# Second layer of a hybrid attention/RWKV-7 kernel: norm behind centring, Gram products earlier, T's blocks turned directly behind them

## The chip, the cores and the metric

The kernel runs on one core of one Trainium2 chip. The metric is the device time of one execution in microseconds (us); the time before is the median of three runs, 2163.39 us (2161.89 to 2163.66). The engines are called PE (matrix multiplications), DVE (VectorE), ACT (ScalarE), POOL (GpSimd) and SP (which issues most loads). Each takes its instructions strictly in the order of the program, and waits at an instruction until what it reads, and the place that it writes, are ready.

## The reference

The reference is a trunk of two residual layers over 512 positions of 2048 channels. Layer 0 is gated differential attention; the change does not touch it. Layer 1 is RWKV-7 time mixing with 32 heads of 64 channels:

```
h = rms_norm(x);  p = h @ w_in;  p = p + (token_shift(p) - p) * mu
r, k, v, g, dw, da = split(p)             # receptance, key, value, gate, decay, rate
for t in range(T):                        # for each head, S is 64 x 64
    sa = S @ a_t
    S  = S * w_t + outer(sa, b_t) + outer(v_t, k_t)
    y_t = S @ r_t
y = (y - mean) * rsqrt(var + eps) * gn_w + gn_b     # over the 64 channels of a head
y = y + sum(r * k * r_k) * v
out = x + (y * silu(g)) @ w_out
```

## The kernel before, in words

Layer 1 goes over 16 pairs of heads, j = 0 to 15; a pair's 128 channels fill the partitions. Each pair needs four projections (keys, receptances, values, gate) of 2048 input channels onto 128 outputs. `proj` makes one out of 48 matmuls of 128x512 into a tile `pp` (16 blocks of input channels, three products each, since both sides are split into a high and a low half; `wh` and `wl` on ACT and DVE make the halves of the weights). These projections are most of PE's work, and all else is hung between their matmuls.

**The recurrence** is done in 8 chunks of 64 positions. For a pair, `gram` makes the products of keys and queries (tile `gp`, 32 matmuls, L1136) from the tiles `BK` and `AR`; ACT copies the 32x32 blocks that the inverse needs to `LP` (L1144) and the rest to `G` (L1150). `t_solve` inverts 64x64 triangular blocks of all chunks at once, which gives T: it turns the blocks on DVE (`LT`, L1214), does 31 steps of elimination on DVE (two instructions each, L1227 and L1230, with tiles `tmpl` and `Tm`), and turns the result twice (`T1`, L1235; `W`, L1240), which POOL copies into `TT` (L1246). `t_first` and `t_second` (PE products into `px`, L1261 and L1276) complete the inverse's lower blocks. POOL's two `affine_select` of each head (`mask_gram`, L1180 and L1182) zero the part of `G` above the diagonal.

**The scan**, `scan_pair`, then goes through the chunks c = 0 to 7. For each: a product of PE into `sm` (L1353), a copy on ACT (`rhs`, L1356), a product (L1366), a copy on ACT (`VS`, L1368), a product (L1373), and on DVE the new state (L1377, for c = 0 L1380), on which the next chunk's L1353 waits. Between them lie fixed counts of `pp` matmuls, the `gaps`: (7, 8) for the full iterations. POOL copies the state into `SA` (L1361) and scales it (L1364). Behind the last chunk come the outputs Y on PE, `centre` (L1410 to L1412 on DVE, result `yc`) and, called from a later place in the loop, `group_norm` (L1420 on ACT, L1422 to L1426 with the helper's lines 63 to 70 on DVE).

**What sets the order.** Iteration j makes the values' projection of pair j (with the Gram products of j behind its 18th matmul, a hook), the keys' projection of j+1, the gate's of j-3 (from j = 3, the constant LAG), and the receptances' projection of j+1 (with masks, `t_first`, `t_second` and the key norms `norms` of a pair as hooks). At the same time the scan of pair j-1 and the elimination of pair j are stepped by a count of PE's matmuls: each `yield n` in `t_solve` or `scan_pair` means that the next piece is bound to the place n matmuls on. That holds for the program's order. The engines wait for data alone, so DVE works the steps off as early as its own queue lets it. Between these bonds the scheduler picks the order on each engine by priority (`AHEAD`, `SCAN`, `SOLVE` raise it).

`soon(g)` runs pieces that were put off until the first `rhs` copy of a chunk; before, it holds the four `G` copies.

Of the kernel before, what the change touches and what calls it, by code (L numbers as in the profile page):

```python
# [1043 lines left out]
    g.nc.tensor.matmul(out, ones, l[:], start=False, stop=True)  # L1044


def soon(g):
    while g.soon:
        g.soon.pop(0)()


def stage1(g, j, k, up):
# [73 lines left out]
def gram(g, j, p):  # L1126

    nc, w, BK = g.nc, g.work, p.BK
    p.G = w.tile([P, NC_, 2, 2, C], F32, name="G1", tag="G1", bufs=2)
    halves = []  # L1130
    for c0, tag in ((0, "pb"), (4, "pc")):
        gp = [g.ps.tile([P, 512], F32, name="gp", tag=tag, bufs=2) for _ in range(2)]
        halves.append((c0, gp))
        for i in range(4):
            for h, r_ in ((0, slice(0, C)), (1, slice(C, P))):
                m = nc.tensor.matmul(gp[h][:, i * P : (i + 1) * P], BK[r_, c0 + i, :, :], p.AR[r_, c0 + i, :, :],  # L1136
                                     start=True, stop=True)
# [9 lines left out]
    def grams():  # L1147
        for c0, gp in halves:
            for h in range(2):
                nc.scalar.copy(p.G[:, c0 : c0 + 4, :, h, :], gp[h][:].rearrange("p (u x t) -> p u x t", u=4, x=2))  # L1150

    g.soon.append(grams)
    if not j:
        soon(g)


def norms(g, j, p, m):
# [49 lines left out]
def t_solve(g, j, p):  # L1207


    nc, w = g.nc, g.work  # L1210
    NQ = HALF // NG
    yield 9
    LT = w.tile([P, HALF, HALF], F32, name="LT", tag="LT", bufs=1)
    lt = nc.vector.transpose(LT[:].rearrange("p (r c) t -> p t r c", r=NG),  # L1214
                        p.LP[:].rearrange("p c t -> p t c")[:, :, None, :].to_broadcast([P, HALF, NG, NC_]))
    Tm = w.tile([P, NQ, HALF], F32, name="Tm", tag="Tm", bufs=1)
    tmp = w.tile([P, NQ * HALF], F32, name="tmpl", tag="tmpl", bufs=1)
    nc.gpsimd.tensor_copy(Tm[:], g.unit[:])
    n2 = p.n2
    behind(g, lt)  # L1220
    with g.tc.issue_after(lt.ins):
        nc.vector.tensor_scalar(n2[:], n2[:], 1e-24, None, ALU.max)
        nc.vector.reciprocal(n2[:], n2[:])
    for i in range(HALF - 1):
        n, s = HALF - 1 - i, i // NG + 1
        tt = tmp[:, : n * s].rearrange("p (a b) -> p a b", a=s)
        st = nc.vector.scalar_tensor_tensor(tt, LT[:, i : i + 1, i + 1 :].to_broadcast([P, s, n]), n2[:, i : i + 1],  # L1227
                                       Tm[:, 0:s, i : i + 1].to_broadcast([P, s, n]), ALU.mult, ALU.mult)
        behind(g, st)
        nc.vector.tensor_add(Tm[:, 0:s, i + 1 :], Tm[:, 0:s, i + 1 :], tt)  # L1230
# [4 lines left out]
    tt = nc.vector.transpose(p.T1[:].rearrange("p c (q r) -> p q r c", r=NG),  # L1235
                        Tm[:].rearrange("p q (r c) -> p q r c", r=NG))
    p.W = w.tile([P, NC_, HALF], F32, name="W", tag="Tm", bufs=1)
    behind(g, tt)
    yield 4
    tt = nc.vector.transpose(p.W[:], p.T1[:])  # L1240
# [101 lines left out]
def scan_pair(g, j, p, gap, gap_s, others):  # L1342
# [8 lines left out]
    for c in range(NC_):  # L1351
        sm = g.ps.tile([P, 512], F32, name="sm", tag="pa", bufs=1)
        nc.tensor.matmul(sm[:, 0:P], both(p.G[:, c, 0]), both(VS[:, c]), start=True, stop=True)  # L1353
# [12 lines left out]
        nc.tensor.matmul(sm[:, P : P + C], both(g.TT[j % 2][:, c]), rhs[:], start=True, stop=True)  # L1366
        for h, r_ in HEADS:
            nc.scalar.copy(VS[r_, c, h, :], sm[r_, P : P + C])  # L1368
        yield gap
        if c == NC_ - 1:  # L1370
            break
        o = P + C
        nc.tensor.matmul(sm[:, o : o + P], p.BKT[:, c, :], both(VS[:, c]), start=True, stop=True)  # L1373
        for h, r_ in HEADS:
            s_ = sm[r_, o + h * C : o + h * C + C]
            if c:
                g.state = nc.vector.scalar_tensor_tensor(VS[r_, c + 1, h, :], s_, p.gam[r_, c : c + 1], Sg[r_, :],  # L1377
                                                         ALU.mult, ALU.add)
            else:
                nc.vector.tensor_scalar(VS[r_, c + 1, h, :], s_, p.gam[r_, c : c + 1], None, ALU.mult)  # L1380
        if c in others:
            others[c]()
        yield gap_s
    outputs(g, j, p)
    centre(g, p)


def outputs(g, j, p):
# [23 lines left out]
        nc.vector.tensor_sub(p.yc[:, h::2, :], yg, s1[:, :, h : h + 1].to_broadcast([P, NT, C]))  # L1412


def group_norm(g, j, p):
    p.chain.finish(g)
    nc, w, yc = g.nc, g.work, p.yc
    NG = 2 * NT
    sq = w.tile([P, NG, C], F32, name="ysq", tag="thg", bufs=1)
    nc.scalar.activation(sq[:], yc[:], AF.Square)  # L1420
    var = g.small.tile([P, NG], F32, name="var", tag="var")
    nc.vector.reduce_sum(var[:], sq[:], AX.X)  # L1422
# [15 lines left out]
def layer1(g, aps):  # L1438
    nc, tc = g.nc, g.tc
    with ExitStack() as cx:  # L1440
# [7 lines left out]
        def proj(i, j, **k):  # L1448
            return unit_chan(g, [(win, i * D + j * P, P)], P, **k)[0]

        def begin(j):
# [5 lines left out]
            pairs.append(stage1(g, j, shift_mix(g, proj(1, j), P, *mus(g, 1, j), "k", 1), up))  # L1457

        def receptances(j):
            def piece(f, i, p):  # L1460
# [2 lines left out]
                        f(g, i, p)  # L1463
                return follow

            behind = [(39, lambda m: norms(g, j, pairs[j], m))]
            if j:
                behind += [(6, lambda m: [mask_gram(g, pairs[j - 1], h, m) for h in range(2)]),
                           (12, piece(t_first, j - 1, pairs[j - 1])), (33, piece(t_second, j - 1, pairs[j - 1]))]
            return shift_mix(g, proj(0, j, behind=behind), P, *mus(g, 0, j), "r", 1)  # L1470

        begin(0)
# [1 line left out]
        for j in range(D // P):  # L1474
            p = pairs[j]
            if j:
# [18 lines left out]
            stage_v(g, j, p, proj(2, j, behind=hooks))  # L1495
            if j == 0:
                turn_keys(g, p, 0)
                turn_keys(g, p, 4)
                turn_values(g, p)
            if j + 1 < D // P:  # L1500
                begin(j + 1)
            if j >= LAG:
                gated(g, j - LAG, pairs[j - LAG], gate(g, j - LAG, proj(3, j - LAG)))
            if j + 1 < D // P:
                r = receptances(j + 1)
                if j:
                    with tc.high_priority(offset=AHEAD):
                        group_norm(g, j - 1, pairs[j - 1])
# [3 lines left out]
        group_norm(g, j - 1, pairs[j - 1])  # L1512
        gts = [gate(g, j - 1, gps)]

        def last_but_one(m):
# [7 lines left out]
        def all_rows(n, _):  # L1523
            if n >= 4 and len(rows) == KT - 2:
                rows.append(split_row(g, gts[0][:]))
            if n >= KT and len(rows) < KT:
                group_norm(g, j, p)
# [59 lines left out]
def body(ctx, tc, nc, aps):  # L1587
    g = Ctx()
    g.nc, g.tc = nc, tc
    g.last, g.first = None, []  # L1590
    g.chains, g.later, g.soon, g.state, g.solve = [], [], [], None, None
# [38 lines left out]
```

## Time and profile before

| what | before |
|---|---|
| median of three runs | 2163.39 us |
| time of the profiled execution | 2163.93 us |
| its span, first to last instruction | 2162.2 us |
| granted PE clock | 0.998 |
| DVE, slices 20 to 35 of the page's 40 (about 1080 to 1945 us) | 80% busy or more |
| first and last Gram products (L1136) start | 1042.3 and 1914.0 us |

The times in the prediction are microseconds from the start of the span of the profiled execution. A row of the timeline reads: start, duration, engine, line, operation, tile written and tiles read with their shapes, how often in a row, and in brackets the time that the engine sat idle before it and what released it. A `pp` matmul shows with 0.39 us, but they overlap: one starts about 0.23 us after the other.

### The profile page before, as it was taken

The page shows a single profiled execution, that of the slowest core. Times are in us where ns is not written, and L with a number is a line of the kernel's source. Part 1 is how long each engine was busy: PE and PEld are TensorE (multiplying, and loading weights), DVE is VectorE, ACT ScalarE, POOL GpSimd, SP SyncE. Part 2 cuts the span into 40 slices and gives each one's busy share as a digit, 9 for nine tenths or more (in the row PEclk, how much of TensorE's full clock was granted, in tenths as well). Part 3 has the DMA queues.
Part 4 walks back from the last instruction along what each step waited for, and adds up shares of the span by engine and source line. Part 5 has one row for each costly group of instructions (what it writes and reads, how often), then busy time and mean ns, then how long its engine had stood idle before and what let it go on. Part 6 is the DMA issues. An engine that isn't in the chain of part 4 may idle for free.

```text
span 2162.2 us, 34954 instructions
## 1 busy us (share of the span) xinstructions
PE 2130.9 (99%) x12260; PEld 1752.8 (81%) x12260; DVE 1547.3 (72%) x4137; ACT 1125.5 (52%) x2587; POOL 335.2 (16%) x614
## 2 busy tenths in 40 slices
PE   9999999999999999999999999999999999999999
PEld 8888888888888878887777888888888888877887
DVE  5665647465656667457888988888888898887645
ACT  6443434343444455345666666666666666655333
POOL 0000000000000000011133322223333322232001
PEclk9999999999999999999999999999999999999999
DMA  6223232322223365663222233222232222345565
GB/s 196 90 86 100 79 99 87 98 89 88 97 88 97 99 198 182 185 139 87 73 69 65 67 81 85 76 77 76 78 85 77 77 68 79 89 118 186 179 169 120
DMA packets 258624, 225.77 MB, mean 104 GB/s; under 512 B 12336, under 2 KB 220480, under 8 KB 258448
## 3 DMA queue, kind: packets, MB, share of 16 engines
q1 hardware_dynamic: 239504, 188.03, 29.2%
q0 software_dynamic: 10080, 19.50, 4.5%
q10 hardware_dynamic: 8864, 16.01, 2.0%
q8 instruction: 96, 1.57, 0.3%
q14 instruction: 80, 0.66, 0.1%
HBM read 207.50 MB, written 15.99 MB: 103 GB/s over the span
## 4 chain that ended last, share of the span: by engine, by line
PE 85%; DVE 11%; issue 2%; ACT 1%; DMA 1%; POOL 0%; DVEq 0%; ACTq 0%; POOLq 0%
PE pp L129 66%; PE pt L129 5%; DVE wl L116 2%; DVE LT L1214 1%; PE sm L1353 1%; PE o L129 1%; PE sc L129 1%; PE lora L129 1%; PE sm L1373 1%; PE sm L1366 1%; DMA yr<-yd 1%; DVE tmpl L1227 1%; PE Y L1395 1%; DVE Tm L1230 1%; PE pt L346 1%
## 5 line engine op out<-in xcount | busy, mean ns | idle before, releaser
L116 DVE TENSOR_TENSOR wl<-wraw,wh 128x512 fp32r<-128x512 f32 (+1 forms) x636 | 446.9, 705 | 383.7 <-ACT wh L115 374.5
L115 ACT CAST wh<-wraw 128x512 fp32r<-128x512 f32 (+1 forms) x636 | 392.9, 619 | 516.9 <-PE pp L129 407.8
L129 PE MATMUL pp<-wh,hH 128*128 128x512 f32 x1268 | 500.3, 395 | 1.2 <-DVE prmin_rw_mu_dram L234 0.6
L129 PE MATMUL pp<-wh,hL 128*128 128x512 f32 x1268 | 497.6, 393 | 0.0
L129 PE MATMUL pp<-wl,hH 128*128 128x512 f32 x1268 | 497.1, 392 | 0.0
L129 PE MATMUL pp<-hH,wh 128*128 128x512 f32 x1024 | 417.7, 408 | 0.0
L129 PE MATMUL pp<-hH,wl 128*128 128x512 f32 x1024 | 413.3, 404 | 0.0
L129 PE MATMUL pp<-hL,wh 128*128 128x512 f32 x1024 | 413.3, 404 | 0.0
L129 PEld LDWEIGHTS pp<-wh,hH 128*128 128x128 f32 x1268 | 238.3, 188 | 50.0 <-issue 1.6
L129 PEld LDWEIGHTS pp<-wh,hL 128*128 128x128 f32 x1268 | 238.2, 188 | 48.6
L129 PEld LDWEIGHTS pp<-wl,hH 128*128 128x128 f32 x1268 | 238.4, 188 | 46.8
L129 PEld LDWEIGHTS pp<-hH,wh 128*128 128x128 f32 x1024 | 193.2, 189 | 37.8 <-issue 2.0
L129 PEld LDWEIGHTS pp<-hH,wl 128*128 128x128 f32 x1024 | 193.6, 189 | 33.4
L129 PEld LDWEIGHTS pp<-hL,wh 128*128 128x128 f32 x1024 | 193.5, 189 | 32.2
L1361 POOL COPY SA<-VS 64x64 f32<-64x64 f32 x224 | 78.0, 348 | 472.6 <-DVE VS L1377 406.9
L1227 DVE SCALAR_TENSOR_TENSOR tmpl<-LT,n,Tm 128x60 f32<-128x60 f32 (+24 forms) x496 | 136.2, 275 | 13.8
L500 POOL DMA_DIRECT2D frow<-yd x12 | 8.9, 743 | 807.6 <-DVE rs_t L67 675.8
L1230 DVE TENSOR_TENSOR Tm<-Tm,tmpl 128x60 f32<-128x60 f32 (+24 forms) x496 | 114.1, 230 | 13.2
L1356 ACT COPY rhs<-sm 64x64 f32<-64x64 f32 x256 | 52.7, 206 | 61.8 <-PE sm L1353 58.9
L1368 ACT COPY VS<-sm 64x64 f32<-64x64 f32 x256 | 53.0, 207 | 59.1 <-PE sm L1366 48.0
L1353 PEld LDWEIGHTS sm<-VS,G 128*128 128x128 f32 x256 | 45.0, 189 | 29.8 <-PE pp L129 12.9
L1377 DVE SCALAR_TENSOR_TENSOR VS<-sm,gam,Sg 64x64 f32<-64x64 f32 x192 | 54.1, 282 | 18.7 <-PE sm L1373 14.2
(339 smaller groups left out, 3261.9 us busy)
## 6 DMA issues: line engine op xcount, KB each, us to landing
wraw<-in_rw_w_in_dram SPq DMA_DIRECT2D x128, 512.0 KB, 4.0
wraw<-in_da_w_in_dram SPq DMA_DIRECT2D x254, 256.0 KB, 3.0
wraw<-in_da_w_out_dram SPq DMA_DIRECT2D x26, 512.0 KB, 4.4
wraw<-in_rw_w_out_dram SPq DMA_DIRECT2D x26, 512.0 KB, 4.1
yr<-yd SPq DMA_DIRECT2D x28, 256.0 KB, 3.4
frow<-yd POOLq DMA_DIRECT2D x12, 512.0 KB, 6.2
xq<-in_x_dram SPq DMA_DIRECT2D x16, 256.0 KB, 5.0
xd<-xq ACTq DMA_DIRECT2D x16, 256.0 KB, 3.9
```

Source lines behind the costliest of these rows:

```text
L115: nc.scalar.copy(hi[:], raw[:, k : k + n])
L116: nc.vector.tensor_sub(lo[:], raw[:, k : k + n], hi[:].bitcast(F32))
L129: m = nc.tensor.matmul(out, a, b, start=s, stop=e, skip_group_check=skip)
L346: nc.tensor.transpose(pt[:, c * P : (c + 1) * P], t1s[t][:, c * P : (c + 1) * P], g.ident[:])
L1214: lt = nc.vector.transpose(LT[:].rearrange("p (r c) t -> p t r c", r=NG), p.LP[:].rearrange("p c t -> p t c")[:, :, None, :].to_broadcast( ...
L1227: st = nc.vector.scalar_tensor_tensor(tt, LT[:, i : i + 1, i + 1 :].to_broadcast([P, s, n]), n2[:, i : i + 1], Tm[:, 0:s, i : i + 1].to_br ...
L1230: nc.vector.tensor_add(Tm[:, 0:s, i + 1 :], Tm[:, 0:s, i + 1 :], tt)
L1353: nc.tensor.matmul(sm[:, 0:P], both(p.G[:, c, 0]), both(VS[:, c]), start=True, stop=True)
L1356: rc = nc.scalar.copy(rhs[r_, :], sm[r_, h * C : h * C + C])
L1361: nc.gpsimd.tensor_copy(p.SA[r_, c - 1, :], VS[r_, c, h, :])
L1368: nc.scalar.copy(VS[r_, c, h, :], sm[r_, P : P + C])
L1377: g.state = nc.vector.scalar_tensor_tensor(VS[r_, c + 1, h, :], s_, p.gam[r_, c : c + 1], Sg[r_, :], ALU.mult, ALU.add)
```

## The change

1. `group_norm` becomes `normal`. It is called at the end of `scan_pair`, right behind `centre`, with raised priority, and no longer after the next receptances. Its buffer `ysq` moves from the place of `thg` to that of `LT`.
2. The Gram products' hook moves from the 18th to the 15th matmul of the values' projection for j of 3 and more (12 for j = 1 and 2, 18 for j = 0, as before).
3. In `t_solve` the pause ahead of the turn `LT` goes from 9 matmuls to 6, and a new pause (9, or 3 for j below 3) stands between `LT` and the first elimination step.
4. The copies of `G` are split in two: the first half goes as before behind the `rhs` copy, the second half (`g.late`) behind the `VS` copy.
5. For j = 0, turning keys and values is hung on matmuls 9, 15 and 27 of the next keys' projection, and no longer stands ahead of it.
6. The key norms' hook of j = 1 moves from 39 to 45, the last iteration's gaps from (4, 5) to (6, 7), and the last pair's scan starts with a delay of 8 and no longer 66.

Every engine has the same instructions before and after. The core of the diff:

```diff
-    g.soon.append(grams)
+    g.soon.append(lambda: grams(*halves[0]))
+    g.late.append(lambda: grams(*halves[1]))
...
-    yield 9
+    yield 6
     LT = w.tile([P, HALF, HALF], F32, name="LT", tag="LT", bufs=1)
...
         nc.vector.reciprocal(n2[:], n2[:])
+    yield 9 if j >= LAG else 3
     for i in range(HALF - 1):
...
-            nc.scalar.copy(VS[r_, c, h, :], sm[r_, P : P + C])
+            vc = nc.scalar.copy(VS[r_, c, h, :], sm[r_, P : P + C])
+        with g.tc.issue_after(vc.ins):
+            soon(g, g.late)
...
     centre(g, p)
+    with g.tc.high_priority(offset=AHEAD):
+        normal(g, p)
...
-def group_norm(g, j, p):
-    p.chain.finish(g)
+def normal(g, p):
+
     nc, w, yc = g.nc, g.work, p.yc
     NG = 2 * NT
-    sq = w.tile([P, NG, C], F32, name="ysq", tag="thg", bufs=1)
+    sq = w.tile([P, NG, C], F32, name="ysq", tag="LT", bufs=1)
...
-            behind = [(39, lambda m: norms(g, j, pairs[j], m))]
+            behind = [(45 if j == 1 else 39, lambda m: norms(g, j, pairs[j], m))]
...
-                gaps = (7, 8) if full else (5, 6) if j == 2 else (4, 5)
+                gaps = (7, 8) if full else (5, 6) if j == 2 else (4, 5) if j == 1 else (6, 7)
...
-            hooks = [(12 if 0 < j < 3 else 18, behind)]
+            hooks = [(12 if 0 < j < LAG else 15 if j else 18, behind)]
...
-                turn_keys(g, p, 0)
-                turn_keys(g, p, 4)
-                turn_values(g, p)
+                turns = ((9, lambda m: turn_keys(g, p, 0)), (15, lambda m: turn_keys(g, p, 4)),
+                         (27, lambda m: turn_values(g, p)))
             if j + 1 < D // P:
-                begin(j + 1)
+                begin(j + 1, turns)
...
-        chain(g, j, p, 66, 5, 6, whole=True)
+        chain(g, j, p, 8, 5, 6, whole=True)
```

The order of the instructions on each engine shows what the scheduler makes of it. **PE, a full iteration, around the Gram products** (`gp`) and chunk 0 of the scan; `pp` rows are the projection. Before:

```order
L1366 MATMUL sm<-rhs,TT_10024 128x64
L129 MATMUL pp<-hL,wh 128x512
...
L129 MATMUL pp<-hL,wh 128x512
L1373 MATMUL sm<-VS,BKT 128x128
L129 MATMUL pp<-hH,wl 128x512
L1136 MATMUL gp<-AR,BK 128x128 x16
L129 MATMUL pp<-hH,wh 128x512
...
L129 MATMUL pp<-hH,wh 128x512
L1353 MATMUL sm<-VS,G_15643 128x128
```

Here 7 `pp` stand between L1366 and L1373, one between L1373 and `gp`, and 7 between `gp` and L1353 of chunk 1. After (the added lines move the numbers: 1366 is 1369, 1373 is 1378, 1136 is 1137, 1353 is 1356):

```order
L1369 MATMUL sm<-rhs,TT_10024 128x64
L129 MATMUL pp<-hL,wh 128x512
...
L129 MATMUL pp<-hH,wl 128x512
L1137 MATMUL gp<-AR,BK 128x128 x16
L129 MATMUL pp<-hH,wh 128x512
L129 MATMUL pp<-hL,wh 128x512
L1378 MATMUL sm<-VS,BKT 128x128
L129 MATMUL pp<-hH,wl 128x512
...
L1356 MATMUL sm<-VS,G_15637 128x128
```

Now 5 `pp` stand ahead of `gp`, two between it and chunk 0's last product, and 8 behind that: `gp` has moved ahead of L1373, three matmuls earlier.

**POOL, a full iteration, behind the state of chunk 5** (`G` is the tile masked, one `affine_select` of 64x8x64 and one of 64x8x128 for each head; `TT` the inverse, `SA` the state's copies). Before:

```order
L1364 TENSOR_SCALAR Sg<-SA,gam 128x64
L1180 AFFINE_SELECT G_15643<-G_15643 64x8x64
L1246 COPY TT_10024<-W 32x8x32 x4
L1361 COPY SA<-VS 64x64
L1182 AFFINE_SELECT G_15643<-G_15643 64x8x128
L1361 COPY SA<-VS 64x64
L1180 AFFINE_SELECT G_15643<-G_15643 64x8x64
L1182 AFFINE_SELECT G_15643<-G_15643 64x8x128
```

After (lines 1182 and 1184 are the masks, 1249 the `TT` copies, 1364 the `SA` copies):

```order
L1367 TENSOR_SCALAR Sg<-SA,gam 128x64
L1182 AFFINE_SELECT G_15637<-G_15637 64x8x64
L1184 AFFINE_SELECT G_15637<-G_15637 64x8x128
L1364 COPY SA<-VS 64x64
L1182 AFFINE_SELECT G_15637<-G_15637 64x8x64
L1364 COPY SA<-VS 64x64
L1249 COPY TT_10024<-W 32x8x32 x4
L1184 AFFINE_SELECT G_15637<-G_15637 64x8x128
```

The first head's long mask now stands directly behind its short one, ahead of the four copies that wait for `W`; the order is the same for every pair from j = 3 on.

**DVE, a full iteration, between the states of chunk 5 and chunk 6** (L1377; the last steps of the elimination, its turns, and pieces of the next pair). Before:

```order
L1377 TENSOR_SCALAR VS<-sm,gam,Sg 64x64 x2
L1435 TENSOR_SCALAR y<-pt,prm_hgw,y 128x512
L1227 TENSOR_SCALAR tmpl<-LT,n_16285,Tm 128x16
...
L1235 STREAM_TRANSPOSE T_16794<-Tm 128x32x8
L116 TENSOR_TENSOR wl<-wraw,wh 128x512
L1240 STREAM_TRANSPOSE W<-T_16794 128x256
L949 TENSOR_SCALAR mixv<-pp,prmin_rw_mu_dram,mixv 128x511
L1377 TENSOR_SCALAR VS<-sm,gam,Sg 64x64 x2
```

After (1382 is the state, 1230 an elimination step, 1238 and 1243 the turns):

```order
L1382 TENSOR_SCALAR VS<-sm,gam,Sg 64x64 x2
L1442 TENSOR_SCALAR y<-pt,prm_hgw,y 128x512
L1230 TENSOR_SCALAR tmpl<-LT,n_16305,Tm 128x24
...
L1238 STREAM_TRANSPOSE T_16808<-Tm 128x32x8
L116 TENSOR_TENSOR wl<-wraw,wh 128x512
L949 TENSOR_SCALAR mixv<-pp,prmin_rw_mu_dram,mixv 128x511
L1382 TENSOR_SCALAR VS<-sm,gam,Sg 64x64 x2
L1243 STREAM_TRANSPOSE W<-T_16808 128x256
```

One step more (of width 24) stands between the two states, and the turn `W` has gone behind the second. At the head of the iteration the norm's 14 instructions on DVE (L1422 to L1426, after: 1429 to 1433) stand ahead of the queries' product `AR` (L1121) where they stood behind L1380, so that `LT` now follows L1380 directly.

More of the change, by code (lines that the diff above doesn't have):

```diff
@@ L1044, in sum_channels, with soon @@
     g.nc.tensor.matmul(out, ones, l[:], start=False, stop=True)
-def soon(g):
-    while g.soon:
-        g.soon.pop(0)()
+def soon(g, pieces=None):
+    pieces = g.soon if pieces is None else pieces
+    while pieces:
+        pieces.pop(0)()
 def stage1(g, j, k, up):
@@ L1145, in gram, with grams @@
                                    gp[h][q : q + HALF].rearrange("p (u x) -> p u x", u=4)[:, :, o : o + HALF])
[L1147 to L1150, printed above, removed]
-    g.soon.append(grams)
+    def grams(c0, gp):
+        for h in range(2):
+            nc.scalar.copy(p.G[:, c0 : c0 + 4, :, h, :], gp[h][:].rearrange("p (u x t) -> p u x t", u=4, x=2))
+    g.soon.append(lambda: grams(*halves[0]))
+    g.late.append(lambda: grams(*halves[1]))
     if not j:
         soon(g)
+        soon(g, g.late)
 def norms(g, j, p, m):
@@ L1367, in scan_pair @@
         for h, r_ in HEADS:
-            nc.scalar.copy(VS[r_, c, h, :], sm[r_, P : P + C])
+            vc = nc.scalar.copy(VS[r_, c, h, :], sm[r_, P : P + C])
+        with g.tc.issue_after(vc.ins):
+            soon(g, g.late)
         yield gap
@@ L1449, in proj, with begin @@
             return unit_chan(g, [(win, i * D + j * P, P)], P, **k)[0]
-        def begin(j):
+        def begin(j, turns=()):
             c0 = j * P
@@ L1456, in begin @@
             up = split_act(g, u[:], w, "up")
-            pairs.append(stage1(g, j, shift_mix(g, proj(1, j), P, *mus(g, 1, j), "k", 1), up))
+            pairs.append(stage1(g, j, shift_mix(g, proj(1, j, behind=turns), P, *mus(g, 1, j), "k", 1),
+                                up))
         def receptances(j):
@@ L1505, in layer1 @@
                 r = receptances(j + 1)
-                if j:
-                    with tc.high_priority(offset=AHEAD):
-                        group_norm(g, j - 1, pairs[j - 1])
-        chain(g, j, p, 66, 5, 6, whole=True)
+        chain(g, j, p, 8, 5, 6, whole=True)
         gated(g, j - 2, pairs[j - 2], gate(g, j - 2, proj(3, j - 2)))
         gps = proj(3, j - 1)
-        group_norm(g, j - 1, pairs[j - 1])
+        pairs[j - 1].chain.finish(g)
         gts = [gate(g, j - 1, gps)]
@@ L1526, in all_rows @@
             if n >= KT and len(rows) < KT:
-                group_norm(g, j, p)
+                p.chain.finish(g)
                 finish_y(g, j, p)
@@ L1590, in body @@
     g.last, g.first = None, []
-    g.chains, g.later, g.soon, g.state, g.solve = [], [], [], None, None
+    g.chains, g.later, g.soon, g.late, g.state, g.solve = [], [], [], [], None, None
     g.const = ctx.enter_context(tc.tile_pool(name="const", bufs=1))
```

4 lines of the change are left out of this document (3 added, 1 removed).

## The prediction

> **What bounds the kernel now.** I read the page's busy times first, then its chain, then PE's waits in layer 1 (line waited for, what released it, us in all, times, longest).
>
> ```profile
> PE 2130.9 (99%) x12260; PEld 1752.8 (81%) x12260; DVE 1547.3 (72%) x4137; ACT 1125.5 (52%) x2587; POOL 335.2 (16%) x614
> ...
> PE 85%; DVE 11%; issue 2%; ACT 1%; DMA 1%; POOL 0%; DVEq 0%; ACTq 0%; POOLq 0%
> ```
>
> ```profile
> PE sm L1353 <- DVE VS L1377: 9.3, 16, 2.2
> PE pt L1303 <- DVE Tm L1230: 3.0, 1, 3.0
> PE sm L1353 <- DVE VS L1380: 2.4, 2, 1.2
> PE px L1261 <- DVE T L1235: 1.9, 3, 0.9
> ```
>
> PE works through the span; no instruction of it goes away, so only its waits can be won or added. In layer 1 they come to some 18 us, 0.8% of the time, nearly all for DVE. The 16 waits of L1353 for the state L1377 split in two: between 1195 and 1870 us there are 12, one in each full iteration (j = 3 to 14).
>
> ```profile
> L1353 PE MATMUL sm<-VS,G x182: 270/274/348, 1196.3 to 1869.3; 128*128 128x128 f32 x182
>   DVE VS L1377: 4.6, 12
> ```
>
> One of them, pair 8's, on PE and on DVE:
>
> ```profile
> 1501.89 0.39 PE L129 MATMUL pp<-hL,wh 128*128 128x512 f32 x1
> 1502.65 0.46 PE L1353 MATMUL sm<-VS,G 128*128 128x128 f32 x2 [0.37 <-DVE VS L1377]
> ```
>
> ```profile
> 1493.15 0.69 DVE L1422 TENSOR_REDUCE var<-ysq 128x8 f32<-128x512 f32 x1
> ...
> 1496.30 0.69 DVE L1426 TENSOR_TENSOR yc<-yc,rsg 128x512 f32<-128x512 f32 x1
> ...
> 1497.52 2.23 DVE L1214 STREAM_TRANSPOSE LT<-LP 128x1024 f32<-128x1024 f32 x1
> ...
> 1501.91 0.60 DVE L1377 SCALAR_TENSOR_TENSOR VS<-sm,gam,Sg 64x64 f32<-64x64 f32 x2
> ```
>
> From the start of the `pp` to L1353 pass 0.76 us where the next matmul usually starts after 0.23: PE loses 0.53, say 0.55. The state is late because `LT` (2.23 us) stands behind the norm's chain (1493.15 to 1496.99, 3.8 us). L1353 starts 0.14 us after the state's end (1502.51).
>
> **The wait that the change aims at.** The norm leaves its place between L1380 and `LT`, so `LT` can follow L1380 as soon as `LP` is copied. The products stand three matmuls earlier (3 x 0.23) and ahead of chunk 0's L1373, which moves behind them; L1380 then ends at about 1495.0 and `LT` runs some 2.5 us earlier than before. One more elimination step (0.5 us) now stands ahead of the state, which leaves about 0.3 us of reserve where 0.55 were missing. The halves of the `G` copies leave ACT (52% busy) with the same work, and `VS` ready sooner. This part takes 12 x 0.55 = **6.6 us** away, bounds 4 to 6.6. I take 6.6, since the chain measured is longer than the wait by far.
>
> **What is late next: the masks on POOL.** Between the states of chunks 5 and 6 there is next to no reserve:
>
> ```profile
> 1473.70 0.42 DVE L1240 STREAM_TRANSPOSE W<-T 128x256 f32<-128x256 f32 x1
> 1474.04 0.71 DVE L949 SCALAR_TENSOR_TENSOR mixv<-pp,prmin_rw_mu_dram,mixv 128x511 f32<-128x511 f32 x1
> 1474.67 0.58 DVE L1377 SCALAR_TENSOR_TENSOR VS<-sm,gam,Sg 64x64 f32<-64x64 f32 x2
> ```
>
> ```profile
> 1475.56 0.38 PE L1353 MATMUL sm<-VS,G 128*128 128x128 f32 x2
> ```
>
> The state ends at 1475.25; with the 0.14 above, L1353 at 1475.56 would have allowed an end at 1475.42, so 0.17 us are spare, and DVE's rows ahead of it show no idle time. Two things are added ahead of this state. One elimination step (0.5 us, by the means of its two instructions in the rows further down) for the turn `W` that goes behind it (0.34 from its start to the next), 0.16 us. And the long mask L1182 of the first head, which stood behind the `TT` copies (1477.40) and now starts straight behind the short one of 1468.94. What a mask does to DVE shows earlier, where a pair's masks ran back to back:
>
> ```profile
> 1116.63 0.65 POOL L1180 TENSOR_SCALAR_AFFINE_SELECT G<-G 64x512 f32<-64x512 f32 x1
> 1117.25 1.16 POOL L1182 TENSOR_SCALAR_AFFINE_SELECT G<-G 64x1024 f32<-64x1024 f32 x1
> ```
>
> ```profile
> 1116.75 0.60 DVE L1227 SCALAR_TENSOR_TENSOR tmpl<-LT,n,Tm 128x54 f32<-128x54 f32 x1
> 1117.38 1.09 DVE L1230 TENSOR_TENSOR Tm<-Tm,tmpl 128x54 f32<-128x54 f32 x1
> ```
>
> ```profile
> L1227 DVE SCALAR_TENSOR_TENSOR tmpl<-LT,n,Tm 128x60 f32<-128x60 f32 (+24 forms) x496 | 136.2, 275 | 13.8
> ...
> L1230 DVE TENSOR_TENSOR Tm<-Tm,tmpl 128x60 f32<-128x60 f32 (+24 forms) x496 | 114.1, 230 | 13.2
> ```
>
> The DVE instructions that start within a mask end with it: the first takes 0.60 us where its group's mean is 0.275, the second 1.09 for 0.23; 0.86 us are lost under the long mask. The same is seen where this mask stands now:
>
> ```profile
> 1468.94 1.19 POOL L1180 TENSOR_SCALAR_AFFINE_SELECT G<-G 64x512 f32<-64x512 f32 x1
> ...
> 1477.40 1.61 POOL L1182 TENSOR_SCALAR_AFFINE_SELECT G<-G 64x1024 f32<-64x1024 f32 x1
> ```
>
> ```profile
> 1477.91 1.11 DVE L1108 TENSOR_TENSOR gam<-m 128x7 f32<-128x7 f32 x1
> ```
>
> `gam`, 7 elements wide, takes 1.11 us and ends with the mask. After the change that loss falls into the full stretch ahead of the state of chunk 6: 0.16 + 0.86 - 0.17 = 0.85 us of wait at the next L1353 in each full iteration, **12 x 0.85 = 10.2 us** (bounds: nothing, if the mask finds a gap of DVE or falls on instructions that it doesn't hold, to 12 x 1.16 = 13.9 for its whole length). I take 0.86, the nearest row. The elimination's end is delayed alike, by 1.4 us (step and mask), to just when PE comes to `px`; that wait lies in the same 0.85.
>
> The Trainium skill ("SBUF — State Buffer", section "Who interferes with whom") says that a VectorE instruction with two SBUF inputs and a GpSimd instruction that reads SBUF shut each other out, for the whole of the one that came first. By that the loss is the mask's full 1.16 and the sum below 3.6 us higher; the trace has 0.86, and the measured row decides.
>
> **The norm ahead of the queries.** The chain of 3.8 us must lie somewhere; it now stands ahead of the queries' product `AR`, on which the products `gp` wait.
>
> ```profile
> 1480.78 1.21 DVE L116 TENSOR_TENSOR wl<-wraw,wh 128x512 fp32r<-128x512 f32 x1 [1.16 <-ACT wh L115]
> ...
> 1484.83 0.69 DVE L116 TENSOR_TENSOR wl<-wraw,wh 128x512 fp32r<-128x512 f32 x1
> 1487.94 0.69 DVE L116 TENSOR_TENSOR wl<-wraw,wh 128x512 fp32r<-128x512 f32 x1 [2.42 <-ACT wh L115]
> ...
> 1489.33 0.69 DVE L1121 TENSOR_TENSOR AR<-mixr,E 128x512 f32<-128x512 f32 x1
> ```
>
> ```profile
> 1492.24 2.06 PE L1136 MATMUL gp<-AR,BK 64*128 64x128 f32 x32
> ```
>
> The gap of 2.42 us hides most of it: 3.8 - 2.4 makes `AR` 1.4 us later, 1491.4, and up to 0.6 more since the chain must first wait for ACT's square. `gp` would be due at 1492.24 less three matmuls (0.68) and L1373 (0.2): 1491.35. So this alone would cost 0.1 to 0.7 us an iteration. But behind a wait of 0.85 at chunk 7 PE comes to `gp` at about 1492.2, when `AR` is there: the two don't add, the longer one counts. The cover lost, it is a rival below. At nothing I cost the buffer of `ysq`: `LT` is read last by the elimination, which is over before `W` (1473.70), 10 us before `yc` is made.
>
> The full iterations thus come to -6.6 + 10.2 = **+3.6 us**.
>
> **The first pair.** Turning the values (L1303) waits for `mixv`, which stands behind elimination steps on DVE:
>
> ```profile
> 1057.55 0.52 PE L1303 MATMUL pt<-ident,mixv 128*128 128x128 f32 x3 [3.01 <-DVE Tm L1230]
> ...
> 1082.95 0.34 PE L1261 MATMUL px<-T,G 32*32 32x32 f32 x10 [0.38 <-DVE T L1235]
> ```
>
> ```profile
> 1055.87 0.74 DVE L949 SCALAR_TENSOR_TENSOR mixv<-pp,prmin_rw_mu_dram,mixv 128x511 f32<-128x511 f32 x1
> ```
>
> Hung behind matmul 27, the turn no longer waits, and 3.2 us of PE's time go. But PE waits for DVE's `T1` at 1082.95 all the same, and DVE works from its `LT` (1046.6 us) to there nearly without a pause; its waits in this stretch are
>
> ```profile
> DVE wl L116 <- ACT wh L115: 1.3, 2, 0.7
> ```
>
> These two shrink when PE runs ahead; the rest moves to `px`. I take **-1.5 us** (bounds 0 and -3.6, the 3.2 with the 0.38). In pairs 1 and 2 (the waits for L1380, two for L1377 of 1.0 and 1.1 us, two of `px`) DVE's order is nearly as before: 0, within 1 either way.
>
> **The last pair.** Three waits:
>
> ```profile
> 1919.10 0.55 PE L1195 MATMUL pt<-ident,BK 128*128 128x128 f32 x3 [0.25 <-ACT G L1150]
> ...
> 1923.16 0.35 PE L1353 MATMUL sm<-VS,G 128*128 128x128 f32 x1 [0.39 <-DVE VS L1377]
> ...
> 1929.98 0.50 PE L1353 MATMUL sm<-VS,G 128*128 128x128 f32 x1 [2.20 <-DVE VS L1377]
> ```
>
> With what a `pp` hides of each they cost 3.3 us. The large one is the four masks again, which start here:
>
> ```profile
> 1923.49 1.00 POOL L1180 TENSOR_SCALAR_AFFINE_SELECT G<-G 64x512 f32<-64x512 f32 x1
> ```
>
> With gaps of 6 and 7 for 4 and 5 matmuls a chunk gets 6 more matmuls, 1.4 us, and the order puts `LT` earlier by the norm's chain. I take **-3.0 us** (bounds -3.3 and -1). The last scan's earlier start fills no wait: behind 1930 the trace shows PE none that counts, so 0.
>
> **The sum.** +3.6 - 1.5 - 3.0 = -0.9 us, against the profiled execution's 2163.93, makes 2163.0. That execution lies 0.54 above the median of the runs, so I forecast **2162.5 us**. A measurement of this kernel tells about 0.2% (4.3 us) from no change; the forecast lies within that.
>
> **The rivals.** *The mask is hidden* (0.27). If it is POOL that is held, or a `wl` that waits for ACT lies beside it, the state of chunk 6 is late by nothing, and the norm's chain ends in time for `gp`: -6.6 - 1.5 - 3.0 = -11.1, 2152.3 us. For it speaks that masks are held too (1.61 and 1.19 us for 1.16 and 0.65), against it that `gam` was held all the same. The Trainium skill's section named above has it that the order of issue decides who blocks; no run here shows that decided.
>
> *The queries come late as well* (0.20), the slower end. Mechanism and place: L1121 behind the norm's chain, ahead of `gp`. If the wait at chunk 7 delays `centre` too, since Y follows on PE, the two waits add: 0.85 + 0.6 - 0.55 = 0.90 an iteration, 10.8 us, and 2163.4 + 10.8 - 4.5 = 2169.7. It decides from the point where `yc` ends later than now, 1484.8. Against it: the `wl` of 1480.78 waited 1.16 us for ACT, which takes up the delay.
>
> *The change doesn't do what it says* (0.07): `LT` is still too late, held by L1380 now behind `gp`, and the wait of 0.55 stays beside the new one. Part of it, half, would give 12 x 0.575 - 4.5 = +2.4, 2165.8; in full 12 x 0.85 - 4.5 = +5.7, 2169.1.
>
> **How the numbers follow.** The forecast has 0.46: 0.34 within 0.2%, 0.07 faster (a mask's cost of half), 0.05 slower (its full length, and no gain in the first pair). The hidden mask's 0.27 is faster, but for 0.01; of the late queries' 0.20, 0.15 slower, 0.05 within; of the last, 0.05 slower, 0.02 within. Faster 0.33, same 0.42, slower 0.25. The forecast's own range is 2158 to 2168; for 8 in 10 it must reach to both rivals: 2151 to 2170.
>
> **What would show it.** In the new trace: no wait of L1353 behind chunk 1 (else the aim failed); one of some 0.7 us (0.85 less what a `pp` hides) behind chunk 6, with a DVE instruction of about 1.1 us under the second mask; no wait of `gp` (else the late queries); L1303 of the first pair without its 3.0, `px` with some 2 of it; the 2.2 of the last pair gone. The forecast is wrong if DVE passes that mask without loss, or if both late waits stand side by side.

## The result, and the profile after

The changed kernel takes **2166.28 us** (median of 20 runs, 2164.74 to 2168.0), the kernel before 2162.89 us in 20 runs on the same chips: ratio 1.0016, 95% interval 1.0009 to 1.0023. It is slower by 3.4 us, where 0.9 us faster was forecast. The profiled execution took 2167.01 us, its span 2165.1.

PE's waits in the full iterations of the changed kernel, between 1195 and 1870 us (line waited for, releaser, us in all, times, longest). In the changed file L1356 is the old L1353, L1382 the state L1377, L1137 the products `gp`, L1122 the queries `AR`, L1264 `px`.

```profile
PE sm L1356 <- DVE VS L1382: 6.0, 11, 0.6
PE gp L1137 <- DVE AR L1122: 5.0, 11, 0.5
PE px L1264 <- DVE T L1238: 1.8, 11, 0.2
```

None of them is the wait behind chunk 1: that has gone. What has come is the wait behind chunk 6 that the prediction had, with a small one of `px` ahead of it, and a third one that it had only as a rival: `gp` waits for the queries. Pair 8 on PE:

```profile
1474.05 0.69 PE L1264 MATMUL px<-T,G 32*32 32x32 f32 x32 [0.15 <-DVE T L1238]
...
1475.72 0.46 PE L1356 MATMUL sm<-VS,G 128*128 128x128 f32 x2 [0.54 <-DVE VS L1382]
...
1492.06 1.16 PE L1137 MATMUL gp<-AR,BK 64*128 64x128 f32 x16 [0.46 <-DVE AR L1122]
```

Against executions without these waits PE loses 0.22, 0.71 and 0.52 us at the three places, 1.45 in all, for 0.55 behind chunk 1 before. From the products of one pair to those of the next an iteration takes 60.86 us, before 59.92.

Where the 2.9 us more of the span lie shows when the start of the same projection matmul (counted from the first) is compared in the two traces:

| at (us, before) | after minus before | what lies between |
|---|---|---|
| 1011 | -0.66 | layer 0, nothing changed |
| 1107 | -2.13 | first pair: -1.5 |
| 1159 | -3.98 | Gram products of pairs 1 and 2: -1.85 |
| 1904 | +6.53 | full iterations: **+10.5** |
| end | +2.91 | last pair and output: -3.6 |

### The profile page after: what moved, and what is told of

Same layout as the page of the kernel before. It is cut to its first block, busy times and chain, and to the rows that moved or that the text cites. A ratio compares the mean times of both kernels' runs of the same rounds, so it can differ in the third digit from the quotient of the medians.

```text
span 2165.1 us, 34929 instructions
## 1 busy us (share of the span) xinstructions
PE 2129.7 (98%) x12260; PEld 1752.7 (81%) x12260; DVE 1557.4 (72%) x4137; ACT 1126.3 (52%) x2587; POOL 337.4 (16%) x614
## 4 chain that ended last, share of the span: by engine, by line
PE 82%; DVE 11%; ACT 3%; issue 3%; DMA 1%; ACTq 0%; DVEq 0%
PE pp L129 63%; PE pt L129 5%; DVE wl L116 2%; PE gp L1137 1%; DVE tmpl L1230 1%; PE o L129 1%; PE sc L129 1%; PE sm L1356 1%; PE lora L129 1%; DVE Tm L1233 1%; PE sm L1378 1%; ACT wh L115 1%; DMA yr<-yd 1%; PE Y L1402 1%; PE sm L1369 1%
## 5 line engine op out<-in xcount | busy, mean ns | idle before, releaser
L1230 DVE SCALAR_TENSOR_TENSOR tmpl<-LT,n,Tm 128x60 f32<-128x60 f32 (+24 forms) x496 | 148.4, 299 | 12.1
L1364 POOL COPY SA<-VS 64x64 f32<-64x64 f32 x224 | 72.4, 323 | 513.2 <-DVE VS L1382 441.6
L1382 DVE SCALAR_TENSOR_TENSOR VS<-sm,gam,Sg 64x64 f32<-64x64 f32 x192 | 54.0, 281 | 30.6 <-PE sm L1378 26.3
L1356 PEld LDWEIGHTS sm<-VS,G 128*128 128x128 f32 x256 | 46.5, 188 | 26.1 <-PE pp L129 13.1
```

## The experiments

Each ratio is to the kernel before, timed along with it; "step" is the time from `gp` to `gp` in a full iteration. The theory at the start: the masks delay DVE ahead of the state of chunk 6, the norm's chain ahead of the queries; open was whether the two add, and why the prediction's cover failed.

**Masks early** (pairs 3 to 14; no engine's order changes but POOL's).

```diff
-                behind += [(6, lambda m: [mask_gram(g, pairs[j - 1], h, m) for h in range(2)]),
+                if not LAG < j:
+                    behind += [(6, lambda m: [mask_gram(g, pairs[j - 1], h, m) for h in range(2)])]
...
+            if j >= LAG:
+                turns = ((36, lambda m: [mask_gram(g, p, h, m) for h in range(2)]),)
```

> The changed kernel with the four masks of pairs 3 to 14 hung behind matmul 36 of the next keys' projection, so that POOL does them some 15 to 20 us earlier; no other engine's order changes. Theory A (the masks and the norm each delay DVE by themselves): the waits of px and of L1356 behind chunk 6 go (0.32 + 0.73 us in 12 iterations), the wait of gp for the queries stays at about 0.6: 12.6 us off 2166.3, about 2153.7. Theory B (as predicted, the longer of two delays counts): the wait of gp grows by what the others lose, about 1.0 to 1.6 us in each iteration, and the time stays within 2 us of 2166. Theory C (the masks feed both, the second head's long one by holding wl ahead of centre): both waits go, 1.67 us in each iteration, about 2147.

2153.64 us, ratio 0.9960 (0.9947 to 0.9972), step 59.75. The time is that of theory A, but not its waits: those of `px`, behind chunk 6 and of `gp` are all gone, as C has it, and a smaller one has come, 0.37 us an iteration, for ACT's `VS`:

```profile
PE sm L1378 <- ACT VS L1371: 1.6, 7, 0.3
```

The masks now hold elimination steps ahead of the state of chunk 4, and what ACT does behind it comes later. So A is refuted by the trace where the time alone would have borne it out.

**Gram products back at 18.**

```diff
-            hooks = [(12 if 0 < j < LAG else 15 if j else 18, behind)]
+            hooks = [(12 if 0 < j < LAG else 18, behind)]
```

> The changed kernel with the Gram products' hook back at matmul 18 for j of 3 and more. If the wait of gp for the queries is only a matter of the three matmuls, it goes (0.62 us in 11 iterations, 6.8 us) and the time is about 2159.5, as long as the state of chunk 1, which has 0.4 us of reserve in the changed kernel, is not late by more. If LT, now later by 0.9 us, makes that state late again (wait of 0.3 to 0.5 us in 12 iterations), 2163 to 2166. The waits of px and behind chunk 6 (0.32 and 0.73) should not change by either.

2213.13 us, ratio 1.0237 (1.0223 to 1.0251): outside all that was expected. PE's waits in layer 1 of this run:

```profile
PE px L1264 <- DVE T L1238: 32.9, 16, 2.6
```

The wait of `gp` is gone, but the elimination's pauses (6 + 9) count from the products, which now come 3 matmuls later, and T1 ends 44.1 us behind the start of `gp` for 42.7. So `px`, whose hook stays, waits 2.5 us for T1 in each full iteration. Hook and pauses are one setting: undone alone, the hook costs some 47 us.

The wait is only half of the loss in an iteration. The step is 61.9 us from pair 3 to pair 4 and 64.8 from pair 5 on, at nearly the same wait. In the trace the granted clock is 0.50 for 6.8 us of each of these later iterations, from just before `px` starts; PE's projection matmuls then come 0.43 us apart for 0.23. From pair 3 to 4 the clock is 1.00 throughout, and in the next iteration it is 0.50 for 3.4 us, with a step of 63.5. All five executions of this kernel have a mean clock of 0.980 to 0.983, those of the kernel before 0.998 to 1.000.

**Norm behind the queries.**

```diff
-    with g.tc.high_priority(offset=AHEAD):
-        normal(g, p)
...
-    sq = w.tile([P, NG, C], F32, name="ysq", tag="LT", bufs=1)
+    sq = w.tile([P, NG, C], F32, name="ysq", tag="thg", bufs=1)
...
+                if j:
+                    with tc.high_priority(offset=AHEAD):
+                        pairs[j - 1].chain.finish(g)
+                        normal(g, pairs[j - 1])
```

> The changed kernel with the norm called behind the receptances and its square in the old buffer, which puts the norm's 14 DVE instructions behind the queries' product but still ahead of the state of chunk 0 and of LT. Theory A and C: the wait of gp goes (0.62 us, 11 times, 6.8 us), and a wait of L1356 for L1385 (chunk 0) comes, 0.5 to 1.0 us, since 3.8 us of DVE now stand ahead of it; with LT later, some of the wait behind chunk 1 may come back. About 2163 to 2170. Waits of px and behind chunk 6 stay at 0.32 and 0.73. Theory B: those two change when the wait of gp goes.

2177.01 us, ratio 1.0066 (1.0054 to 1.0079), step 61.46. PE's waits in layer 1, and the end of the norm on DVE:

```profile
PE sm L1356 <- DVE VS L1385: 13.6, 14, 1.5
PE sm L1356 <- DVE VS L1382: 10.9, 17, 1.2
```

```profile
1438.85 0.69 DVE L1431 TENSOR_TENSOR yc<-yc,rsg 128x512 f32<-128x512 f32 x1
1439.46 0.59 DVE L1385 TENSOR_SCALAR VS<-sm,gam 64x64 f32<-64x64 f32 x2
```

The wait of `gp` goes (0.52 us), the state of chunk 0 (L1385), now behind the norm, is late by 1.14 us in each iteration, and the wait behind chunk 6 doesn't move. The sum is above the range named: by the same matmuls as in the table, this run takes 7.7 us more than the changed kernel in the full iterations, 1.8 in pair 2, and 1.65 in the last pair; the last two were not expected. That the norm's chain stands on the path to the queries is shown; so is that the wait behind chunk 6 has nothing to do with it.

**First and last pair alone** (parts 5 and 6 on the kernel before: turns of pair 0 as hooks, key norms of pair 1 at 45, last gaps 6 and 7, delay 8).

> The kernel before with only parts 5 and 6 of the change (turns of pair 0 hung into the next keys' projection, key norms of pair 1 at 45, last gaps 6 and 7, last delay 8). Prediction's terms: 1.5 us less in the first pair and 3.0 in the last, so 4.5 below the kernel before, about 2158.4, with the 12 waits behind chunk 1 of 0.55 us unchanged. If the 1.8 us that the changed kernel also gains around the Gram products of pair 2 come from these parts too, 6.3 below, 2156.6; if the gain in the last pair comes from the earlier LT and not from the gaps, 2161.

2159.43 us, ratio 0.9987 (0.9978 to 0.9996). By the same matmuls the first pair wins 2.0 us, the pairs 1 and 2 nothing, the last pair 1.0: there the wait of the state under the four masks has stayed.

```profile
PE sm L1353 <- DVE VS L1377: 9.4, 15, 2.5
```

So the 1.85 us of pair 2 do not come from these parts. Before, pair 2 lost 1.36 us of them where PE waited 1.2 us for the state of chunk 0; after, that wait is not there. It is the norm's move: the run with the norm behind the queries wins 0.07 there, the one with parts 2 and 3 undone, further down, 1.96.

The last pair's 1.0 has another source. In the profiled execution of the kernel before, the granted clock is 0.50 for 3.4 us from 1930.0, behind the wait of 2.2 us, and PE's projection matmuls come 0.42 us apart for 0.23: some 1.6 us lost. This run has no such stretch there, though its wait is longer (2.48 us). So, by the traces, its gaps alone won nothing in the last pair.

**Second head's long mask away.** The long masks go into a function `mask_long`, which `mask_gram` skips for the heads in `p.put_off`; `scan_pair` does them one iteration later:

```diff
+            if c == 1:
+                for h in getattr(p, "put_off", ()):
+                    mask_long(g, p, h)
...
+            if LAG <= j < D // P - 1:
+                p.put_off = (1,)
```

> The changed kernel with the long mask of the second head alone (pairs 3 to 14) done one iteration later, behind the first Sg of the pair's own scan, beside LT; it is needed only by the outputs Y. Theory C (this mask, by holding the wl that stands ahead of centre, makes the queries late): that wl takes 0.7 us and no longer 1.6, yc and the queries come 0.9 us earlier, the wait of gp (0.62, 11 times) goes, the waits of px and behind chunk 6 (0.32 + 0.73, 12 times) stay: about 2159.5. Theory A (the norm's chain makes the queries late by itself): the wait of gp stays, 2166. As the prediction had it (the longer counts): no change either.

2164.63 us, ratio 1.0005 (0.9996 to 1.0014), step 60.64. DVE ahead of `centre` and at the queries:

```profile
1479.32 0.69 DVE L116 TENSOR_TENSOR wl<-wraw,wh 128x512 fp32r<-128x512 f32 x1 [0.57 <-ACT wh L115]
...
1489.10 0.69 DVE L1122 TENSOR_TENSOR AR<-mixr,E 128x512 f32<-128x512 f32 x1
```

`wl` takes 0.69 where the changed kernel has 1.64, and the wait of `gp` (0.52) is gone, while those of `px` and behind chunk 6 stay: C. The time is higher than expected because the mask costs 0.31 us in its new place, ahead of the state of chunk 1.

**First head's long mask away** (`p.put_off = (0,)`, and the second head's masks at hook 18).

> The changed kernel with the long mask of the first head alone done one iteration later, and both masks of the second head hung at matmul 18, so that they stand behind the TT copies. Theory C: the waits of px and behind chunk 6 go (1.05 us, 12 times); the masks that are left hold the DVE instructions ahead of centre as before, a little more by the short one (0.3), so the wait of gp stays at 0.6 to 0.9: 2154 to 2158. As the prediction had it (the longer counts): the wait of gp grows to 1.6 and the time stays at 2166.

2158.08 us, ratio 0.9979 (0.9969 to 0.9988), step 60.20. POOL and DVE ahead of `centre`:

```profile
1475.45 1.61 POOL L1180 TENSOR_SCALAR_AFFINE_SELECT G<-G 64x1024 f32<-64x1024 f32 x1
```

```profile
1475.95 1.64 DVE L917 TENSOR_TENSOR sLx<-k,sHx 128x512 fp32r<-128x512 f32 x1
...
1486.25 0.69 DVE L1122 TENSOR_TENSOR AR<-mixr,E 128x512 f32<-128x512 f32 x1
```

The waits of `px` and behind chunk 6 are gone (0.92 us), that of `gp` stays as it was, though PE arrives 0.92 us earlier: it neither grew, as "the longer counts" demands, nor shrank. The queries move with the state of chunk 6, and the mask that is left holds `sLx` (1.64 for 0.69). The mask put off costs 0.25 us in its new place, ahead of the state of chunk 1.

**Both long masks away** (`p.put_off = (0, 1)`).

> The changed kernel with the long masks of both heads done one iteration later beside LT. Theory C: all three waits go (1.05 us 12 times, 0.62 us 11 times), as long as the masks beside LT, which has one input from the same memory, hold nothing: 2147. Theory A: the wait of gp stays, 2153.7. If the masks hold the first elimination steps instead, the state of chunk 1 with its reserve of 0.37 us is late by up to 0.6 us, 12 times: 2154.

2157.64 us, ratio 0.9973 (0.9962 to 0.9984), step 60.10. `px` and `gp` don't wait; 0.26 us are lost at chunk 1 and 0.40 stay behind chunk 6 (0.29 of them recorded as idle time), under the two short masks. The masks did not come to lie beside `LT` (1432.52 to 1434.75):

```profile
1437.43 2.73 POOL L1180 TENSOR_SCALAR_AFFINE_SELECT G<-G 64x1024 f32<-64x1024 f32 x2 [4.02 <-ACT G L1150]
```

They waited, and hold the `wl` ahead of the state of chunk 1 (1.23 us for 0.69). Whether `LT` would be held was thus not tried.

**Both long masks away, on the kernel before** (the same edit).

> The kernel before with the long masks of both heads moved the same way. There the state behind chunk 6 has 0.18 us of reserve and the queries 2 us, so nothing is won there. Behind the first Sg the masks fall on the norm's chain ahead of LT, by up to 2.3 us; half of its instructions have two inputs. If they are held, LT and the state of chunk 1 are later and its wait of 0.55 us grows by 0.5 to 2 us: 2169 to 2187. If not, 2163.

2173.33 us, ratio 1.0045 (1.0032 to 1.0057). The loss behind chunk 1 grows from 0.55 to 1.37 us, 12 times. That is the whole of the longer step (60.77 for 59.92): taking the two masks away from their old place won nothing, and here they cost 10 us.

**Parts 2 and 3 undone** (hook 18, pause 9, no pause behind `LT`; the norm stays early).

```diff
-    yield 6
+    yield 9
...
-    yield 9 if j >= LAG else 3
...
-            hooks = [(12 if 0 < j < LAG else 15 if j else 18, behind)]
+            hooks = [(12 if 0 < j < LAG else 18, behind)]
```

> The changed kernel with parts 2 and 3 undone (Gram products at matmul 18, one pause of 9 ahead of LT, none behind); the norm's earlier place, the split copies, first and last pair stay. POOL's order is then that of the kernel before: the four TT copies ahead of the first long mask. If parts 2 and 3 bring the two late waits (by the mask's place and by the three matmuls), both go, the wait behind chunk 1 stays away since LT no longer follows the norm: 59.4 us an iteration for 59.92 before and 60.86 after, in all about 2150. If the norm's place alone makes the queries late, a wait of gp of 0.3 to 0.6 stays: 2153 to 2156. If LT, 0.9 us later than in the changed kernel, lets the wait behind chunk 1 come back: up to 2157.

2154.21 us, ratio 0.9963 (0.9950 to 0.9975), step 59.84. Neither `px`, nor chunk 6, nor `gp` waits; behind chunk 1 some 0.45 of the 0.55 us stay:

```profile
1435.64 0.46 PE L1355 MATMUL sm<-VS,G 128*128 128x128 f32 x2 [0.30 <-DVE VS L1381]
```

So parts 2 and 3 bring both late waits and take the early one away. Without them the change wins 12 x 0.1 us in the full iterations, 3.9 in the first pairs and 2.3 in the last one by the same matmuls (with them 3.3 and 3.6), and pays nothing for it.

**Long masks spread**: one ahead of the state of chunk 2, one ahead of chunk 4, one iteration later; the second head's short mask at hook 18.

```diff
+            if c in (2, 4) and getattr(p, "put_off", ()):
+                behind(g, mask_long(g, p, c // 2 - 1))
...
+                late = 18 if j > LAG else 6
+                behind += [(6, lambda m: mask_gram(g, pairs[j - 1], 0, m)), (late, lambda m: mask_gram(g, pairs[j - 1], 1, m)),
```

> The changed kernel with the two long masks of pairs 3 to 14 done one iteration later, one ahead of the state of chunk 2 and one ahead of that of chunk 4, where the changed kernel has 1.15 and 1.26 us of reserve, and the second head's short mask behind the TT copies. Each long mask costs DVE 0.9 us where it lies, less than the reserve, so all the waits of the full iteration go: 59.4 us, about 2149 in all. If the second one delays what ACT does ahead of VS of chunk 5, as in the run with early masks, 0.2 to 0.4 us stay: 2152.

**2150.28 us, ratio 0.9941 (0.9927 to 0.9954)**, step 59.44: PE has no recorded wait between 1195 and 1870 us. The masks hold DVE as before, as here:

```profile
1448.77 1.16 POOL L1180 TENSOR_SCALAR_AFFINE_SELECT G<-G 64x1024 f32<-64x1024 f32 x1
```

```profile
1448.83 1.18 DVE L1239 TENSOR_TENSOR Tm<-Tm,tmpl 128x70 f32<-128x70 f32 x1
```

They do it where the state has more than 1 us of reserve. This is the best version found, 12.4 us under the kernel before and 16.0 under the changed one's median above.

**Blank masks**: the long masks of pairs 3 to 14 become memsets (`nc.gpsimd.memset(p.G[r_, :, 1], 0.001)`) at the places of the changed kernel. This kernel leaves that part of the masking out and serves for its time alone.

> The changed kernel in which the long masks of pairs 3 to 14 are replaced by memsets of the same size at the same places; they write and read nothing, and that part of the masking is left out of the computation. If it is POOL's reading that holds DVE, the instruction beside the first one takes 0.2 to 0.3 us (1.12 now), wl 0.7 (1.64 now), the waits of px, behind chunk 6 and of gp go as in the run with both long masks away, without its cost behind chunk 1: about 59.5 us an iteration, 2151. If any work of POOL on the same memory holds DVE, the waits stay as far as the memset is as long as the mask: 2160 to 2166.

2150.48 us, ratio 0.9944 (0.9930 to 0.9957), step 59.46. The first memset, and DVE's instruction that starts within it:

```profile
1463.24 0.94 POOL L1185 MEMSET G<- 64x1024 f32 x1
```

```profile
1463.85 0.22 DVE L1233 SCALAR_TENSOR_TENSOR tmpl<-LT,n,Tm 128x16 f32<-128x16 f32 x1
```

0.22 us, at the place where the changed kernel has 1.12. POOL is busy for 0.94 us in place of 1.16 and writes the same bytes; what it no longer does is read. Under all 24 memsets no DVE instruction lasts over 0.02 us longer than usual. The order on PE, DVE and ACT is that of the changed kernel, and all three waits are gone. So what the change costs in the full iterations comes from the two masks in their new place.

## Why the prediction was wrong, point by point

1. **The wait aimed at: right, its reason only in part.** The 12 waits behind chunk 1 are gone, 0.55 us each. The prediction took the whole 0.55 because the norm's chain of 3.8 us leaves. With parts 2 and 3 undone the chain has left too, and 0.45 of the 0.55 stay: DVE then idles 1.74 us shortly ahead of `LT`, which starts 4.7 us behind the start of `gp` for 5.3 before. In the changed kernel it starts 3.6 us behind. It takes the earlier products and the moved pauses as well.
2. **The mask ahead of the state of chunk 6: right in place and kind, 0.93 us for 0.85.** POOL and DVE in the changed kernel:

```profile
1468.19 1.20 POOL L1182 TENSOR_SCALAR_AFFINE_SELECT G<-G 64x512 f32<-64x512 f32 x1
1469.35 1.69 POOL L1184 TENSOR_SCALAR_AFFINE_SELECT G<-G 64x1024 f32<-64x1024 f32 x1
...
1480.37 1.16 POOL L1184 TENSOR_SCALAR_AFFINE_SELECT G<-G 64x1024 f32<-64x1024 f32 x1
```

```profile
1466.73 0.60 DVE L1382 SCALAR_TENSOR_TENSOR VS<-sm,gam,Sg 64x64 f32<-64x64 f32 x2
...
1469.95 1.12 DVE L1230 SCALAR_TENSOR_TENSOR tmpl<-LT,n,Tm 128x16 f32<-128x16 f32 x1
...
1480.43 1.64 DVE L116 TENSOR_TENSOR wl<-wraw,wh 128x512 fp32r<-128x512 f32 x1 [0.57 <-ACT wh L115]
...
1484.06 0.74 DVE L1419 TENSOR_TENSOR yc<-Y,s 128x256 f32<-128x256 f32 x2
1485.50 0.69 DVE L1429 TENSOR_REDUCE var<-ysq 128x8 f32<-128x512 f32 x1 [0.70 <-ACT ysq L1427]
...
1491.32 0.69 DVE L1122 TENSOR_TENSOR AR<-mixr,E 128x512 f32<-128x512 f32 x1
```

   The elimination step beside the long mask takes 1.12 us for 0.23: 0.89 lost, for the 0.86 taken. The Trainium skill's sentence in "SBUF — State Buffer", "Who interferes with whom", that an instruction of VectorE with two SBUF inputs contends with a GpSimd instruction "that reads SBUF, not with one that only writes it", is borne out by the run with memsets (0.22 us beside 0.94). In the rows shown, an instruction that starts together with a long mask lost 0.86 to 0.95 us of the mask's 1.16. `wl` starts only 0.06 us after its mask and lost 0.95, so a later start explains little of the difference; the rest is open.

3. **"The two don't add, the longer one counts": this step failed.** From the end of `yc` to the end of `AR` DVE needs 7.2 us for 5.3 before, 1.9 more, of which the prediction had 1.4 to 2.0. But the end of `yc` itself, measured from the start of the state of chunk 5, comes at 18.07 us for 17.24: 0.83 us later. Before, these two stood at

```profile
1467.48 0.60 DVE L1377 SCALAR_TENSOR_TENSOR VS<-sm,gam,Sg 64x64 f32<-64x64 f32 x2
...
1483.96 0.76 DVE L1412 TENSOR_TENSOR yc<-Y,s 128x256 f32<-128x256 f32 x2
```

   The prediction named this as the point from which the rival decides, and put it aside because `wl` (1480.78) waited 1.16 us for ACT, "which takes up the delay". It takes up less than it meets: the wait shrinks to 0.57 us, and `wl` starts 0.40 us later from the state of chunk 5, since ACT's copy of `VS`, `k` and `wh` follow PE, which waited behind chunk 6:

```profile
1478.70 0.44 ACT L1371 COPY VS<-sm 64x64 f32<-64x64 f32 x2 [0.22 <-issue]
1479.16 0.72 ACT L1107 ACTIVATE k<-mixk,prm_kk 128x512 f32<-128x512 f32 x1
1479.79 0.60 ACT L115 CAST wh<-wraw 128x512 fp32r<-128x512 f32 x1
```

   And it lasts 1.64 us for 1.21: the second head's long mask, which the new order puts behind the `TT` copies (1480.37 in the rows above), lies squarely on it. Before, this mask began half a microsecond ahead of `wl` and held it for only the rest:

```profile
1480.29 1.17 POOL L1182 TENSOR_SCALAR_AFFINE_SELECT G<-G 64x1024 f32<-64x1024 f32 x1
```

   The order of POOL's instructions ahead of the prediction showed that mask's move; the prediction priced the first head's alone. Each part was tried by itself: without the second long mask the wait of `gp` goes and that behind chunk 6 stays, without the first it is the other way round.

4. **The full iterations** thus come to -12 x 0.55 + 12 x 0.93 + 11 x 0.52 = +10.3 us, +10.5 by the traces, for a predicted +3.6. It is the late queries' rival (+10.8) that took place, given 0.20, though it had the delay of `centre` come by PE and Y alone, and half of it came by the second mask.
5. **The first pair: right**, -1.5 predicted and measured; L1306 (the old L1303) no longer waits, and the rest moves on to `px` and to the state behind it (page of all waits in layer 1):

```profile
PE px L1264 <- DVE T L1238: 4.8, 15, 1.3
PE sm L1356 <- DVE VS L1385: 1.4, 1, 1.4
PE pt L1044 <- DVE sLx L917: 1.0, 1, 1.0
```

6. **Pairs 1 and 2: mis-sized**, 0 within 1 predicted, -1.85 measured. The prediction took DVE's order in these pairs to be nearly as before, but the norm's move takes away a wait for the state L1380 there, worth 1.36 us.
7. **The last pair: right in size**, -3.0 predicted, -3.6 measured, but not as it was worked out. Some 1.6 us of it are the stretch of half clock behind the wait of 2.2 us, which the profiled execution before has and the one after has not; the prediction's 3.3 us had waits alone. The gaps alone won nothing of it. What is left there:

```profile
1933.56 0.46 PE L1356 MATMUL sm<-VS,G 128*128 128x128 f32 x2 [0.41 <-DVE VS L1382]
1936.08 0.43 PE L1369 MATMUL sm<-rhs,TT 128*128 128x64 f32 x2 [0.69 <-ACT rhs L1359]
```

The terms outside the full iterations were too cautious by 2.4 us, the full iterations too low by 6.9; that makes the 4.3 us by which the forecast missed, but for layer 0's scatter. That both mistakes partly cancel is luck: with the full iterations alone off, the time would have been some 2169 us, above the forecast's own range (2158 to 2168).

## What to carry to other kernels

When a change moves many instructions on one engine, go through every one that moved on every engine, the second of a pair too: the price of one mask was worked out exactly and that of its twin not at all. Two waits for one engine that works nearly without a pause can add. Whether they do is decided by the idle time of that engine between them, counted from the last instruction that both waits share, and by all that is put into it: here 1.16 us of idle time did not cover the delay, as a second mask came to lie behind it. And where POOL must read and write large tiles, put it where DVE's next due result has the most reserve: by the place of the masks alone, the changed kernel takes 2150 or 2166 us.

## What was not expected of the hardware

A memset of POOL of 0.94 us holds no DVE instruction, at the very place where an `affine_select` of 1.16 us holds one for 0.9. The prediction spoke of the masks as such and had no use for the difference. It is the cheapest of the findings to use: of the DVE instructions that start under the 24 memsets none was held. Other POOL instructions that only write were not tried here.

A wait of PE can cost more than itself. Behind some waits of 2.2 to 3.0 us the traces here show the granted clock at 0.50 for 3.4 or 6.8 us, and this doubled the price of the wait of `px` in the run with the products at 18. It doesn't come each time: the 3.0 us wait in the first pair of the kernel before was followed by a clock of 1.00, the same wait in the run with both long masks away on that kernel by 3.4 us at 0.50. What decides is not shown.
